# Windowed attention with a context prefix: the products across the border of the two token halves made for two heads at once

## The chip, the core and the metric

The kernel runs on one core of one Trainium2 chip. The core's engines work side by side and wait for each other through semaphores: PE multiplies matrices (PEld is the loading of its stationary operand), DVE and ACT work element by element and can read PE's results, POOL works element by element on the on-chip memory alone, and SP issues most of the DMAs. The metric is the device time of one execution in microseconds (us).

## The reference

Two layers run over 1,024 latent tokens of width 1,024 and 256 context tokens: an attention layer, then a convolution layer, then a final norm. The change lies in the attention layer, whose core is this:

```python
def windowed_attention(q, k, v, kc, vc, sink):
    # 16 query heads, 4 key/value heads, head width 128, WINDOW = BLOCK = 128
    ...
    def block_fn(args):
        qblk, blk = args                       # one block of 128 queries
        kw = lax.dynamic_slice_in_dim(kp, start, span, axis=1)   # keys of 3 blocks
        vw = lax.dynamic_slice_in_dim(vp, start, span, axis=1)
        ...
        p_ctx, p_win = sink_softmax(sink_l, s_ctx, s_win)
        o = (jnp.einsum('bhgqc,bchd->bqhgd', p_ctx.astype(vc.dtype), vc)
             + jnp.einsum('bhgqk,bkhd->bqhgd', p_win.astype(vw.dtype), vw))
        return o
    ...
y = (o * jax.nn.silu(z)) @ w_out
```

A block of 128 queries reads the key blocks before it, at it and behind it, and all 256 context keys, in one softmax with a sink. The result is multiplied by a gate made from z before the output projection.

## The kernel before

Every fp32 operand is held as two parts, a rounded high part and the rest as low part, and a product is three matmuls: high by high, low by high, high by low. All matmuls of the attention are issued in the order in which the program is written; the instructions of the other engines, SP's DMA issues among them, are ordered by a scheduler.

The attention walks 128 steps, 16 heads (h) by 8 query blocks (qb). In a step PE makes the scores of the next step (`scores`, L1035), then a fixed number of matmuls of other work, usually 12 (`fill`, L1022: projections of later heads, at the end the first rows of the output projection), then, where one is queued, a product of probabilities and values (`pv`, L1090), then the transposes of this step's probabilities (`transposes`, L1069). Between `scores` and `transposes` the softmax runs on the other engines: DVE takes scores, mask and maximum into p, ACT the exponential, DVE the reciprocal, POOL scales p.

`transposes` leaves the probability blocks, keys in the partitions, in two buffers of 22 blocks of 128 columns: `pthi` (high parts, written by ACT) and `ptlo` (low parts, DVE). They serve one token half, that is 4 query blocks, at a time, and the next half writes over them.

`pv(h, half)` multiplies the blocks of one half by the values. It makes seven products of three matmuls each, all into one PSUM bank (`pso`, 512 columns): two for the context, 512 columns wide; four for the half's own key blocks, 256 or 384 wide; and one for the key block just across the border between the halves. That last one concerns one query block alone, 128 columns. It is made 256 wide: the query block's probabilities stand beside a block of `pthi` and `ptlo` that was set to zero at the program's start (blocks 0 and 21). DVE then multiplies the bank by the gate into `oz`, and SP stores 512 columns to `ozd` in DRAM. The half 0 of a head is queued after step qb = 3 and made in step 4; the half 1 is made in step 0 of the next head. Where the next head begins a new group of four, keys and values are made first and `pv(h, 1)` stands behind them (L1220 on).

The output projection (`proj_attn`, L720) reads `ozd` back in rows of two heads (`ozf`, split by ACT into `ozh` and by DVE into `ozl`) with the weights `wo` and `wol`. The first `EARLY_ROWS` = 7 rows are begun for two token blocks inside the last head's steps; `ahead` (L753) loads up to `EA` = 2 rows ahead.

Tiles of 1,024 words come from a list of 45 pages that are handed out in the order in which they were freed (`Pages`). Operations are recorded through one helper, so the profile puts nearly all of them on L89; they are told apart by the names of their tiles.

Of the kernel before, what the change touches and what calls it, by code (L numbers as in the profile page):

```python
# [19 lines left out]
NH = 16  # L20
# [74 lines left out]
def backbone_kernel(  # L95
# [526 lines left out]
    anchor = []  # L622
    anchor_p = []
    anchor_a = []

    def after(ins, anchor=anchor):
        if anchor:
# [92 lines left out]
    def proj_attn():  # L720

        st, oz = {}, {}
        todo = {"load": 0, "split": 0}

        def load(i):
            s, kk = seqB[i]
            h, m = subs[s]
            w, wl = pg.alloc(F32, [2, 512], "wo"), pg.alloc(F32R, [2, 512], "wol")
            SY.dma_start(out=w, in_=pair_rows(Wo, m, kk))
            SY.dma_start(out=wl.bitcast(F32), in_=wolA[m, kk])  # L730
            st[i] = [w, wl]
            if m == 0:
                f = pg.alloc(F32, [2, 512], "ozf")
                SY.dma_start(out=f, in_=ozd[2 * kk:2 * kk + 2, :, h * 512:h * 512 + 512].rearrange("a p n -> p a n"))
                oz[(h, kk)] = f

        def split(i):
            s, kk = seqB[i]
            h, m = subs[s]
            w, wl = st[i]  # L740
            wh = pg.alloc(F32R, [2, 512], "woh")
            act(wh, w, AF.Copy)
            pg.free(w)
            st[i] = (wh, wl)
            if m == 0:
                f = oz[(h, kk)]
                oh, ol = pg.alloc(F32R, [2, 512], "ozh"), pg.alloc(F32R, [2, 512], "ozl")
                act(oh, f, AF.Copy)
                split_lo(V, ol, f, oh)
# [186 lines left out]
    def finish(kind, n, half, o, d, ropes=None, hold=None):  # L936
# [10 lines left out]
        if kind in "qk":  # L947
            return rope(o, sl, d, ropes, hold)
        if kind == "z":
            act(d[:, sl], o, AF.Tanh, scale=0.5)  # L950
            stt(d[:, sl], d[:, sl], 1.0, o, ALU.add, ALU.mult)
            return None
        w = CT if half == 2 else 512
        f = hp.alloc(F32, None, "vf")
# [80 lines left out]
    def scores(h, qb):  # L1035
# [29 lines left out]
        V.reciprocal(ri, l0)  # L1065
        anchor_p[:] = [G.tensor_scalar(out=p[:, 0:w], in0=p[:, 0:w], scalar1=ri, scalar2=1.0, op0=ALU.mult, op1=ALU.mult)]
        ptile[(h, qb)] = p

    def transposes(h, qb):  # L1069
        p = ptile.pop((h, qb))  # L1070
# [1 line left out]
        nb = k1 - k0 + 1  # L1072
        tb = ps_s()
        ql = qb % 4
        rels = []
        for kb in range(k1, k0 - 1, -1):
            rel = 1 - (kb - qb)
            rels.append(rel)
            PE.transpose(tb[:, rel * P:(rel + 1) * P], p[:, (kb - k0) * P:(kb - k0 + 1) * P], ident)
        for i in range(2):  # L1080
            PE.transpose(tb[:, (3 + i) * P:(4 + i) * P], p[:, (nb + i) * P:(nb + i + 1) * P], ident)
# [8 lines left out]
    def pv(h, half):  # L1090
        g = h // 4
        c, vh, vl = kvt[g][2:5]
        o = ps_o(0)
        q0 = half * 4
        work = [(*(c[:, n, i * P:i * P + P] for n in (2, 3)), slice(13 + 4 * i, 17 + 4 * i), slice(0, 512)) for i in range(2)]
        for kb in range(max(q0 - 1, 0), min(q0 + 4, TB - 1) + 1):
            qa, qz = max(kb - 1, q0), min(kb + 1, q0 + 3)
            b0 = 1 + 4 * (1 - (kb - qa)) + (qa - q0)
            n = qz - qa + 1
            if n == 1 and kb > qa:  # L1100
                work.append((vh[:, kb], vl[:, kb], slice(0, 5, 4), slice(256, 512)))
            elif n == 1:
                work.append((vh[:, kb], vl[:, kb], slice(9, 22, 12), slice(0, 256)))
            else:
                work.append((vh[:, kb], vl[:, kb], slice(b0, b0 + 5 * (n - 1) + 1, 5),
                             slice((qa - q0) * P, (qz - q0 + 1) * P)))
        for n, (a, b, ps_, os_) in enumerate(work):
            last = n == len(work) - 1
            PE.matmul(o[:, os_], a, pthi[:, ps_], start=n == 0, stop=False)
            PE.matmul(o[:, os_], a, ptlo[:, ps_], start=False, stop=False)  # L1110
            PE.matmul(o[:, os_], b, pthi[:, ps_], start=False, stop=last)
        sl = slice(half * 512, half * 512 + 512)
        oz = hp.alloc(F32, None, "oz")
        stt(oz[:, 0:512], o, 0.5, zt[h][:, sl], ALU.mult, ALU.mult)
        SY.dma_start(out=ozd[h, :, sl], in_=oz[:, 0:512])
        hp.free(oz)
        if half:
            pg.free(zt.pop(h))
            pg.free(*qt.pop(h))

    d0 = [target("k", 0), [], []]
    tails = []
# [73 lines left out]
    for i, (h, qb) in enumerate(steps):  # L1196
# [22 lines left out]
        if regroup:  # L1219
# [3 lines left out]
            transposes(h, qb)  # L1223
            run(job(("v", g)))
            pv(h, 1)
            pg.free(*old)
            scores(*nxt)
            vlate.pop(g)()
            continue
# [14 lines left out]
    pg.free(*kvt[NG - 1])  # L1244
    pg.free(mask_pg)


# [624 lines left out]
```

## Time and profile before

| | us |
|---|---|
| median of 3 runs | 1698.68 |
| lowest and highest of them | 1698.52 and 1701.01 |
| the profiled execution's own time | 1698.45 |
| its span in the trace | 1696.5 |

In the profile, rows of grouped instructions give line, engine, operation, tiles (written from read), shape and count, then the busy time in us and the mean duration of one in ns, then the engine's idle time before them and what ended it. Rows of the timeline give the start in us, the duration, and the instruction. A matmul's duration runs from its start to its modelled end; matmuls overlap, so the duration of one is longer than the distance to the next.

### The profile page before, as it was taken

The numbers are of one execution on the slowest core, as the hardware profiler recorded it, in microseconds if no ns is written. First come the engines' busy times: TensorE is split into PE (matmuls) and PEld (weight loads), VectorE is DVE, ScalarE is ACT, GpSimd is POOL, SyncE is SP. The second block draws the span as 40 slices with busy tenths as digits, with TensorE's granted clock in tenths as the row PEclk, the third lists the DMA queues.
The fourth block names the chain that finished last, engine by engine and source line by source line (L and its number), as shares of the span: only waits on it lengthen the run. The fifth ranks groups of instructions, "written<-read, shape, count | busy, mean of one in ns | idle before, by whom it ended". The sixth has DMA issues, their size and how long they took to land.

```text
span 1696.5 us, 23980 instructions
## 1 busy us (share of the span) xinstructions
PE 1682.6 (99%) x8484; PEld 1419.0 (84%) x8484; DVE 1088.4 (64%) x2068; ACT 877.4 (52%) x1540; POOL 880.8 (52%) x730
## 2 busy tenths in 40 slices
PE   9999999999999999999999999999999999999998
PEld 6788888888888888888888888888888888888886
DVE  5755544555355544556215289999999999867832
ACT  5745543555355544546234355665665664566741
POOL 0255663666556663653001167999898888130400
PEclk9999999999999999999999999999999999999999
DMA  9424442444335443437776623010111202377881
GB/s 386 147 82 134 158 122 94 134 143 152 97 119 160 149 134 93 140 120 279 269 253 219 234 81 100 13 63 26 63 62 44 88 32 81 125 267 247 312 296 50
DMA packets 110424, 244.55 MB, mean 144 GB/s; under 512 B 11370, under 2 KB 28066, under 8 KB 110304
## 3 DMA queue, kind: packets, MB, share of 16 engines
q1 hardware_dynamic: 104224, 233.05, 40.4%
q10 hardware_dynamic: 6080, 9.97, 2.3%
q8 instruction: 67, 1.10, 0.3%
q14 instruction: 53, 0.43, 0.1%
HBM read 190.80 MB, written 41.69 MB: 137 GB/s over the span
## 4 chain that ended last, share of the span: by engine, by line
PE 94%; DMA 3%; DVE 1%; POOL 1%; ACT 1%; issue 0%; SPq 0%; ACTq 0%; POOLq 0%
PE psg L89 49%; PE pss L89 24%; PE pso L89 21%; DMA x_page<-in_x_dram 1%; DMA rope_half<-rope_half 1%; DMA x_page<-in_ctx_dram 1%; DMA araw_page<-in_k_ada_dram 1%; DVE hf_page L89 0%; POOL rope_half L89 0%; DMA dww_raw<-in_ada_w_dram 0%; POOL wlo_page L89 0%; ACT x_page L89 0%; ACT hh_page L89 0%; DVE hl_page L89 0%; POOL ql_page L89 0%
## 5 line engine op out<-in xcount | busy, mean ns | idle before, releaser
L89 POOL TENSOR_TENSOR odd_half<-odd_half,prod_half 128x513 f32<-128x513 f32 (+2 forms) x252 | 314.1, 1253 | 22.7 <-ACT prod_half L89 9.4
L89 PE MATMUL psg<-hh_page,whi_page 128*128 128x512 f32 x600 | 235.5, 393 | 0.0
L89 PE MATMUL psg<-hl_page,whi_page 128*128 128x512 f32 x600 | 234.4, 391 | 0.0
L89 PE MATMUL psg<-hh_page,wlo_page 128*128 128x512 f32 x600 | 234.0, 390 | 0.0
L89 POOL TENSOR_TENSOR wlo_page<-wraw_page,whi_page 128x512 fp32r<-128x512 f32 (+1 forms) x104 | 173.0, 1678 | 106.7 <-ACT whi_page L89 55.9
L89 ACT ACTIVATE prod_half<-ubuf,dww 128x513 f32<-128x513 f32 (+2 forms) x252 | 165.5, 675 | 116.4 <-POOL odd_half L89 112.5
L89 PE MATMUL psg<-h2h_page,whi_page 128*128 128x512 f32 x464 | 181.9, 392 | 0.0
L89 PE MATMUL psg<-h2h_page,wlo_page 128*128 128x512 f32 x464 | 180.6, 389 | 0.0
L89 PE MATMUL psg<-h2l_page,whi_page 128*128 128x512 f32 x464 | 180.6, 389 | 0.0
L89 POOL TENSOR_SCALAR p_page<-p_page,sc 128x640 f32<-128x640 f32 (+1 forms) x128 | 99.2, 775 | 143.2 <-DVE sc L89 135.1
L89 DVE SCALAR_TENSOR_TENSOR pss<-ubuf,dww,pss 128x512 f32<-128x512 f32 (+3 forms) x270 | 172.3, 670 | 0.1
L89 DVE SCALAR_TENSOR_TENSOR pss<-ubuf,wsum,pss 128x512 f32<-128x512 f32 (+3 forms) x270 | 171.7, 670 | 0.2
L89 ACT ACTIVATE pthi<-pss 128x640 fp32r<-128x640 f32 (+1 forms) x144 | 89.2, 619 | 140.1 <-PE pss L89 130.1
L89 DVE TENSOR_TENSOR ptlo<-pss,pthi 128x640 fp32r<-128x640 f32 (+1 forms) x144 | 103.3, 718 | 82.4 <-ACT pthi L89 81.9
L89 ACT ACTIVATE p_page<-p_page,sc 128x641 f32<-128x641 f32 (+1 forms) x128 | 102.8, 803 | 70.1 <-DVE sc L89 67.5
L89 PEld LDWEIGHTS psg<-hh_page,wlo_page 128*128 128x128 f32 x600 | 112.7, 188 | 24.5
L89 POOL TENSOR_TENSOR rope_half<-rope_half,sin_page 128x512 f32<-128x512 f32 x40 | 52.9, 1322 | 153.3 <-DMA rope_half<-rope_half 147.1
L89 PEld LDWEIGHTS psg<-hh_page,whi_page 128*128 128x128 f32 x600 | 112.7, 188 | 19.3
L89 PEld LDWEIGHTS psg<-hl_page,whi_page 128*128 128x128 f32 x600 | 112.8, 188 | 18.4
L89 ACT ACTIVATE whi_page<-wraw_page 128x1024 fp32r<-128x1024 f32 x88 | 92.6, 1052 | 54.2 <-PE psg L89 21.0
L89 PE MATMUL pso<-h2l_page,whi_page 128*128 128x512 f32 x304 | 118.3, 389 | 0.0
L89 PE MATMUL pso<-h2h_page,wlo_page 128*128 128x512 f32 x304 | 118.3, 389 | 0.0
(255 smaller groups left out, 4056.0 us busy)
## 6 DMA issues: line engine op xcount, KB each, us to landing
wraw_page<-in_k_wconv_dram SPq DMA_DIRECT2D x48, 512.0 KB, 3.3
wraw_page<-in_k_win_dram SPq DMA_DIRECT2D x40, 512.0 KB, 3.4
wol_page<-wolA SPq DMA_DIRECT2D x32, 512.0 KB, 6.2
wo_page<-in_attn_w_out_dram SPq DMA_DIRECT2D x32, 512.0 KB, 6.0
wo_page<-in_conv_w_out_dram SPq DMA_DIRECT2D x32, 512.0 KB, 6.3
wol_page<-wolC SPq DMA_DIRECT2D x32, 512.0 KB, 6.1
rope_half<-rope_half ACTq DMA_DIRECT2D x76, 128.0 KB, 3.2
araw_page<-in_k_ada_dram SPq DMA_DIRECT2D x16, 512.0 KB, 11.0
```

Source lines behind the costliest of these rows:

```text
L89: r = f(*a, **k)
```

## The change

- The border product leaves `pv`, which then has six products, and no zero blocks are needed. For each pair of heads (2n, 2n + 1) one new function, `pv_shared`, makes the border products of both heads and both directions: key block 4 with the query blocks 3 of both heads (256 columns), and key block 3 with the query blocks 4 of both heads (256 columns). It stands in step qb = 2 of the next pair's even head, and for the last pair behind the last `pv`.
- For that the even head's border blocks are kept in blocks 20 and 21 of `pthi` and `ptlo` until the odd head's are there, in blocks 3 and 16. The other blocks are laid out anew, so that the two-piece copy of step qb = 0 becomes one piece, and that of the even head's steps 3 and 4 becomes two.
- `pv` stores 384 columns to `ozd` in place of 512. The 128 columns of the border block, which lack the products across the border, are copied by DVE into a page (`ozs`, 1,024 words), and ACT copies the gate's columns of the two border blocks of a head there too. `pv_shared` multiplies its bank by these gate columns (two DVE operations of 128 by 256), adds the kept sums (one of 128 by 512), and stores 256 columns for each of the two heads.
- Pages: one more is held for a pair's sums and gates; a group's two value pages are freed two steps later; a head's two query pages are freed earlier, in the last `scores` of the head.
- In the output projection the early rows no longer load rows 7 and 8, since row 7 reads heads 14 and 15, whose border columns are stored last. The splits of `ozf` in later rows are ordered behind the last gate computation (`anchor_z`).

The diff, cut:

```diff
-    for t in (pthi, ptlo):
-        for b in (0, 21):
-            V.tensor_copy(t[:, b], zer[:, 0:P])
...
-            ahead(i, EA, min(1, EARLY_ROWS - 1 - i))
+            ahead(i, min(EA, EARLY_ROWS - 1 - i), min(1, EARLY_ROWS - 1 - i))
...
-        for r0, r1 in (((0, 2), (3, 5)) if qb == 0 else ((1, 5),) if qb == TB - 1 else ((0, 5),)):
-            b0 = 1 + ql + 4 * r0
-            bs = slice(b0, b0 + 4 * (r1 - r0 - 1) + 1, 4)
+        a0, a1 = int(qb == TB - 1), 4 if qb == 0 else 5
+        runs = [(a0, a1, slice(ql + 4 * a0, ql + 4 * a1 - 3, 4))]
+        if h % 2 == 0 and qb == 3:
+            runs = [(1, 5, slice(7, 20, 4)), (0, 1, slice(20, 21))]
+        elif h % 2 == 0 and qb == 4:
+            runs = [(0, 4, slice(0, 13, 4)), (4, 5, slice(21, 22))]
+        for r0, r1, bs in runs:
             anchor_a[:] = [act(pthi[:, bs], tv[:, r0:r1], AF.Copy)]
+        for r0, r1, bs in runs:
             anchor[:] = [split_lo(V, ptlo[:, bs], tv[:, r0:r1], pthi[:, bs])]
...
-        for kb in range(max(q0 - 1, 0), min(q0 + 4, TB - 1) + 1):
+        for kb in range(q0, q0 + 4):
...
-            if n == 1 and kb > qa:
-                work.append((vh[:, kb], vl[:, kb], slice(0, 5, 4), slice(256, 512)))
-            elif n == 1:
-                work.append((vh[:, kb], vl[:, kb], slice(9, 22, 12), slice(0, 256)))
...
-        SY.dma_start(out=ozd[h, :, sl], in_=oz[:, 0:512])
+        stt(oz[:, 0:512], o, 0.5, zv, ALU.mult, ALU.mult)
+        V.tensor_copy(part[:, e0:e0 + 128], oz[:, edge])
+        SY.dma_start(out=ozd[h, :, sl][:, own], in_=oz[:, own])
         hp.free(oz)
         if half:
+            act(part[:, 768 - 256 * (h % 2):1024 - 256 * (h % 2)], zt[h][:, 384:640], AF.Copy)
             pg.free(zt.pop(h))
...
+    def pv_shared(h):
+        vh, vl = kvt[h // 4][3:5]
+        o = ps_o(0)
+        pv_mm(o[:, 0:256], [(vh[:, 4], vl[:, 4], slice(3, 21, 17), slice(0, 256))])
+        pv_mm(o[:, 256:512], [(vh[:, 3], vl[:, 3], slice(16, 22, 5), slice(0, 256))])
+        part = shared.pop()
+        oz = hp.alloc(F32, None, "oz")
...
+        for e in range(2):
+            stt(sv[:, e], ov[:, e], 0.5, zv[:, e], ALU.mult, ALU.mult)
+        tt(V, oz[:, 0:512], oz[:, 0:512], part[:, 0:512], ALU.add)
+        for e in range(2):
+            SY.dma_start(out=ozd[h - e, :, 384:640].rearrange("p (q n) -> p q n", q=2), in_=sv[:, e])
...
+        if qb == 1 and h and h % 2 == 0:
+            pvq.append((h - 1, 2))
...
+    fill(12)
+    pv(NH - 1, 2)
     fill(1000)
```

What it does to the order of instructions is shown at three places. On PE, the end of one `pv` (head 4, half 0; `pso` is its bank, `vh` and `vl` the values' two parts), before:

```order
L89 MATMUL pso_2978<-pthi,vh_page_2619 128x384
L89 MATMUL pso_2978<-ptlo,vh_page_2619 128x384
L89 MATMUL pso_2978<-pthi,vl_page_2620 128x384
L89 MATMUL pso_2978<-pthi,vh_page_2619 128x256
L89 MATMUL pso_2978<-ptlo,vh_page_2619 128x256
L89 MATMUL pso_2978<-pthi,vl_page_2620 128x256
L89 MATMUL pso_2978<-pthi,vh_page_2619 128x256
L89 MATMUL pso_2978<-ptlo,vh_page_2619 128x256
L89 MATMUL pso_2978<-pthi,vl_page_2620 128x256
```

and now the new product of heads 2 and 3, two steps ahead of that place, between the fill and the transposes of its step:

```order
L89 MATMUL psg_2840<-hl_page_500,whi_page_2646 128x512
L89 MATMUL psg_2840<-hh_page_499,wlo_page_2647 128x512
L89 MATMUL pso_2890<-pthi,vh_page_777 128x256
L89 MATMUL pso_2890<-ptlo,vh_page_777 128x256
L89 MATMUL pso_2890<-pthi,vl_page_778 128x256
L89 MATMUL pso_2890<-pthi,vh_page_777 128x256
L89 MATMUL pso_2890<-ptlo,vh_page_777 128x256
L89 MATMUL pso_2890<-pthi,vl_page_778 128x256
L89 MATMUL pss_2903<-ident,p_page_2815 128x128 x5
```

Each of the 32 `pv` has lost three rows of 256 columns, the border product (last in half 0, first behind the context in half 1), and each of the 8 pairs has gained six; nothing else on PE has changed its place.

On POOL, around the scaling of head 2, step 3 (`p_page`; `wlo` is the low part of a projection weight that the scheduler put in between, `low` that of an output weight), before:

```order
L89 TENSOR_SCALAR p_page_1812<-p_page_1812,sc_1813 128x640
L89 TENSOR_TENSOR wlo_page_1948<-wraw_page_1541,whi_page_1947 128x512 x2
L89 TENSOR_SCALAR p_page_1853<-p_page_1853,sc_1854 128x640
L89 TENSOR_TENSOR low_page_1839<-low_page_1839,lhi_page_1389 128x512
L89 TENSOR_SCALAR p_page_1896<-p_page_1896,sc_1897 128x640
```

and now:

```order
L89 TENSOR_TENSOR low_page_1674<-low_page_1674,lhi_page_1383 128x512
L89 TENSOR_SCALAR p_page_1801<-p_page_1801,sc_1802 128x640
L89 TENSOR_SCALAR p_page_1842<-p_page_1842,sc_1843 128x640
L89 TENSOR_TENSOR wlo_page_1952<-wraw_page_1535,whi_page_1951 128x512 x2
L89 TENSOR_TENSOR low_page_1828<-low_page_1828,lhi_page_1383 128x512
```

The two halves of the weight's low part now stand behind the scaling of step 3 and no longer ahead of it.

On SP, at the end of the attention (`oz_half` is what a `pv` leaves, `ozf` what a row of the output projection reads), before:

```order
L89 DMA ozf_page_8074<-ozd 128x2x512
L89 DMA wol_page_8286<-wolA 128x1024
L89 DMA dwr_page_8139<-in_conv_dw_w_dram 31x1024
L89 DMA gate_page_8136<-gd_603 128x1024
L89 DMA wo_page_8285<-in_attn_w_out_dram 128x2x512
L89 DMA wo_page_8465<-in_attn_w_out_dram 128x2x512
L89 DMA ozd<-oz_half_8116 128x512
L89 DMA xr_page_8470<-in_x_dram 128x512 x2
```

and now:

```order
L89 DMA ozd<-oz_half_8155 128x384
L89 DMA wol_page_8324<-wolA 128x1024
L89 DMA ozd<-oz_half_8179 128x2x128 x2
L89 DMA wo_page_8323<-in_attn_w_out_dram 128x2x512
L89 DMA ozf_page_8309<-ozd 128x2x512
L89 DMA wo_page_8405<-in_attn_w_out_dram 128x2x512
L89 DMA xr_page_8530<-in_x_dram 128x512 x2
```

The load of row 7's input (the `ozf` row of each) stood ahead of the last store of the attention; it now stands behind the two stores of the last pair's border columns, which it needs.

More of the change, by code (lines that the diff above doesn't have):

```diff
@@ L624, in backbone_kernel @@
     anchor_a = []
+    anchor_z = []
     def after(ins, anchor=anchor):
@@ L747, in split @@
                 oh, ol = pg.alloc(F32R, [2, 512], "ozh"), pg.alloc(F32R, [2, 512], "ozl")
-                act(oh, f, AF.Copy)
-                split_lo(V, ol, f, oh)
+                after(act(oh, f, AF.Copy), anchor_z[0:1] if i else [])
+                after(split_lo(V, ol, f, oh), anchor_z[1:2] if i else [])
                 pg.free(f)
@@ L1067, in scores @@
         ptile[(h, qb)] = p
+        if qb == TB - 1:
+            pg.free(*qt.pop(h))
     def transposes(h, qb):
@@ L1074, in transposes @@
         ql = qb % 4
-        rels = []
         for kb in range(k1, k0 - 1, -1):
-            rel = 1 - (kb - qb)
-            rels.append(rel)
-            PE.transpose(tb[:, rel * P:(rel + 1) * P], p[:, (kb - k0) * P:(kb - k0 + 1) * P], ident)
+            at = 2 - 2 * (kb - qb)
+            PE.transpose(tb[:, at * P:(at + 1) * P], p[:, (kb - k0) * P:(kb - k0 + 1) * P], ident)
         for i in range(2):
-            PE.transpose(tb[:, (3 + i) * P:(4 + i) * P], p[:, (nb + i) * P:(nb + i + 1) * P], ident)
+            at = 1 + 2 * i
@@ L1087, in transposes @@
+        for r0, r1, bs in runs:
             anchor_a[:] = [act(pthi[:, bs], tv[:, r0:r1], AF.Copy)]
+        for r0, r1, bs in runs:
             anchor[:] = [split_lo(V, ptlo[:, bs], tv[:, r0:r1], pthi[:, bs])]
[L1090 to L1095, printed above, removed]
-        for kb in range(max(q0 - 1, 0), min(q0 + 4, TB - 1) + 1):
-            qa, qz = max(kb - 1, q0), min(kb + 1, q0 + 3)
-            b0 = 1 + 4 * (1 - (kb - qa)) + (qa - q0)
-            n = qz - qa + 1
-            if n == 1 and kb > qa:
-                work.append((vh[:, kb], vl[:, kb], slice(0, 5, 4), slice(256, 512)))
-            elif n == 1:
-                work.append((vh[:, kb], vl[:, kb], slice(9, 22, 12), slice(0, 256)))
-            else:
-                work.append((vh[:, kb], vl[:, kb], slice(b0, b0 + 5 * (n - 1) + 1, 5),
-                             slice((qa - q0) * P, (qz - q0 + 1) * P)))
+    shared = []
@@ L1107, in pv, with pv_mm @@
+    def pv_mm(o, work):
         for n, (a, b, ps_, os_) in enumerate(work):
@@ L1111, in pv @@
             PE.matmul(o[:, os_], b, pthi[:, ps_], start=False, stop=last)
+    def pv(h, half):
+        if half == 2:
+            return pv_shared(h)
+        c, vh, vl = kvt[h // 4][2:5]
+        o = ps_o(0)
+        q0 = half * 4
+        work = [(*(c[:, n, i * P:i * P + P] for n in (2, 3)), slice(4 + 8 * i, 8 + 8 * i), slice(0, 512)) for i in range(2)]
+        for kb in range(q0, q0 + 4):
+            qa, qz = max(kb - 1, q0), min(kb + 1, q0 + 3)
+            b0 = qa - q0 + 8 * (qa - kb + 1)
+            work.append((vh[:, kb], vl[:, kb], slice(b0, b0 + 9 * (qz - qa) + 1, 9), slice((qa - q0) * P, (qz - q0 + 1) * P)))
+        pv_mm(o, work)
@@ L1112, in pv @@
         sl = slice(half * 512, half * 512 + 512)
+        if h % 2 == 0 and half == 0:
+            shared[:] = [pg.alloc(F32, [1024], "ozs")]
+        part = shared[0]
         oz = hp.alloc(F32, None, "oz")
-        stt(oz[:, 0:512], o, 0.5, zt[h][:, sl], ALU.mult, ALU.mult)
-        SY.dma_start(out=ozd[h, :, sl], in_=oz[:, 0:512])
+        own, edge = (slice(128, 512), slice(0, 128)) if half else (slice(0, 384), slice(384, 512))
+        zv = zt[h][:, sl]
+        e0 = 256 * half + 128 * (1 - h % 2)
@@ L1116, in pv @@
+        stt(oz[:, 0:512], o, 0.5, zv, ALU.mult, ALU.mult)
+        V.tensor_copy(part[:, e0:e0 + 128], oz[:, edge])
+        SY.dma_start(out=ozd[h, :, sl][:, own], in_=oz[:, own])
         hp.free(oz)
         if half:
+            act(part[:, 768 - 256 * (h % 2):1024 - 256 * (h % 2)], zt[h][:, 384:640], AF.Copy)
             pg.free(zt.pop(h))
-            pg.free(*qt.pop(h))
+    def pv_shared(h):
+        vh, vl = kvt[h // 4][3:5]
+        o = ps_o(0)
+        pv_mm(o[:, 0:256], [(vh[:, 4], vl[:, 4], slice(3, 21, 17), slice(0, 256))])
+        pv_mm(o[:, 256:512], [(vh[:, 3], vl[:, 3], slice(16, 22, 5), slice(0, 256))])
+        part = shared.pop()
+        oz = hp.alloc(F32, None, "oz")
+        ov, sv, pv_ = (t[:, 0:512].rearrange("p (q e n) -> p e q n", q=2, e=2) for t in (o, oz, part))
+        zv = part[:, 512:1024].rearrange("p (e q n) -> p e q n", q=2, e=2)
+        for e in range(2):
[3 more added lines that the diff above has]
+            SY.dma_start(out=ozd[h - e, :, 384:640].rearrange("p (q n) -> p q n", q=2), in_=sv[:, e])
+        hp.free(oz)
+        pg.free(part)
+        if h % 4 == 3:
+            pg.free(vh, vl)
@@ L1225, in backbone_kernel @@
             pv(h, 1)
-            pg.free(*old)
+            pg.free(*old[:3])
             scores(*nxt)
@@ L1242, in backbone_kernel @@
         pv(*pvq.popleft())
+    fill(12)
+    pv(NH - 1, 2)
     fill(1000)
-    pg.free(*kvt[NG - 1])
+    pg.free(*kvt[NG - 1][:3])
     pg.free(mask_pg)
```

4 lines of the change are left out of this document (2 added, 2 removed).

## The prediction

> **What bounds the kernel now.** I read the page first: the share of each engine and the chain of work that ended last.
>
> ```profile
> span 1696.5 us, 23980 instructions
> PE 1682.6 (99%) x8484; PEld 1419.0 (84%) x8484; DVE 1088.4 (64%) x2068; ACT 877.4 (52%) x1540; POOL 880.8 (52%) x730
> ...
> PE 94%; DMA 3%; DVE 1%; POOL 1%; ACT 1%; issue 0%; SPq 0%; ACTq 0%; POOLq 0%
> ```
>
> PE is on the chain for 94% of the span. A busy PE need not be a bound one, so the second view is that of the waits, for PE alone (engine, what waited, for whom: us in total, times, longest):
>
> ```profile
> PE pss L89 <- DVE zerr_page L89: 2.0, 1, 2.0
> PE psg L89 <- DVE rope_half L89: 1.4, 2, 1.1
> ...
> PE pso L89 <- DVE oz_half L89: 0.5, 3, 0.2
> ```
>
> The first is the start-up's. The other two, 1.9 us together, are all that matters here: in the attention PE hardly waits. The third view, busy time by stretch (attention, output projection, convolution), says whether another engine is close behind (columns: stretch, its length, then PE, PEld, DVE, ACT and POOL busy, granted clock, DMA share, GB/s):
>
> ```profile
> 100.00:825.00 725.00, 723.09 (x4021) 628.91 (x4020) 370.87 (x818) 354.39 (x741) 396.50 (x368) 1.00 0.44 140
> 825.00:870.00 45.00, 45.00 (x209) 36.87 (x208) 7.21 (x17) 14.35 (x19) 2.97 (x2) 1.00 0.78 260
> ...
> 1100.00:1500.00 400.00, 400.00 (x1773) 331.10 (x1772) 387.75 (x591) 235.20 (x321) 316.45 (x217) 1.00 0.21 69
> ```
>
> In the attention the other engines are busy for half of the time or a little more, so PE work that is removed there is time. DVE is close behind only in the convolution (387.75 of 400), whose work the change leaves as it is: it starts earlier and runs as before.
>
> **What is removed.** The border product is three matmuls in each of 32 `pv`, 96 in all; the 8 shared products bring back six each, 48. So 48 matmuls of 256 columns go. Their price is not the duration in the grouped rows:
>
> ```profile
> L89 PE MATMUL pso<-ptlo,vh_page 128*128 128x256 f32 x96 | 26.9, 281 | 0.0
> L89 PE MATMUL pso<-pthi,vl_page 128*128 128x256 f32 x96 | 26.9, 281 | 0.0
> ```
>
> 281 ns is start to modelled end, and neighbours overlap. What PE's line advances by is the distance from start to start, in the timeline of one `pv`:
>
> ```profile
> 165.05 0.28 PE L89 MATMUL pso<-pthi,vh_page 128*128 128x256 f32 x1
> 165.16 0.28 PE L89 MATMUL pso<-ptlo,vh_page 128*128 128x256 f32 x1
> 165.28 0.28 PE L89 MATMUL pso<-pthi,vl_page 128*128 128x256 f32 x1
> 165.40 0.28 PE L89 MATMUL pso<-pthi,vh_page 128*128 128x256 f32 x1
> 165.51 0.28 PE L89 MATMUL pso<-ptlo,vh_page 128*128 128x256 f32 x1
> 165.63 0.28 PE L89 MATMUL pso<-pthi,vl_page 128*128 128x256 f32 x1
> 165.75 0.34 PE L89 MATMUL pso<-pthi,vh_page 128*128 128x384 f32 x1
> ```
>
> Six of them take 165.75 − 165.05 = 0.70 us, 0.117 each. The last three are such a padded border product, so the price is that of the very form. 48 x 0.117 = **5.6 us** off PE's line. (By durations it would be 48 x 0.281 = 13.5, which PE's own line contradicts.)
>
> **What is added beside it.** Rows for the new operations, the nearest ones:
>
> ```profile
> L89 DVE SCALAR_TENSOR_TENSOR pso<-wsum_raw,cs,pso 128x256 f32<-128x256 f32 x64 | 30.7, 480 | 3.3 <-DMA wsum_raw<-in_ada_w_dram 3.2
> L89 DVE TENSOR_TENSOR x_page<-x_page,xr_page 128x512 f32<-128x512 f32 x20 | 14.9, 743 | 0.3
> L89 DVE COPY mask_page<-pso 128x256 f32<-128x256 f32 x16 | 6.7, 420 | 0.2
> L89 DVE TENSOR_TENSOR ptlo<-pss,pthi 128x640 fp32r<-128x640 f32 x96 | 78.8, 821 | 57.8 <-ACT pthi L89 57.5
> L89 DVE TENSOR_TENSOR ptlo<-pss,pthi 128x256 fp32r<-128x256 f32 x32 | 13.5, 421 | 6.9 <-ACT pthi L89 6.6
> L89 DVE TENSOR_TENSOR ptlo<-pss,pthi 128x512 fp32r<-128x512 f32 x16 | 11.0, 690 | 17.8 <-ACT pthi L89 17.8
> L89 ACT ACTIVATE pthi<-pss 128x256 fp32r<-128x256 f32 x32 | 12.3, 384 | 29.9 <-PE pss L89 23.6 <-DVE ptlo L89 6.3
> ```
>
> DVE, for a pair: four copies of 128 columns, at most 0.42 each (a row of twice the width), 1.7; two gate products, 2 x 0.48, and one addition, 0.74, together 1.70; the splits of step 0 in one piece, 0.69 for 2 x 0.42, save 0.15 for each of two heads; those of the even head's steps 3 and 4 in two pieces, 0.69 + at most 0.42 for 0.82, cost 0.29 each. Sum about 3.7 us, 8 pairs 29 us, beside 371 of 725. ACT gets two gate copies of 0.38 a pair and like changes of its splits, some 8 us in all, beside 354. SP gets 16 more stores of the same bytes. None of this is on PE's line as long as the softmax of the next step is done in time.
>
> That cover has to be looked at where it is thinnest. A step's transposes wait for POOL's scaling of p, and the new DVE work stands in step 2 of even heads, ahead of the transposes of step 3. Two such places, head 2 and head 6, POOL and PE:
>
> ```profile
> 175.85 2.56 POOL L89 TENSOR_TENSOR wlo_page<-wraw_page,whi_page 128x512 fp32r<-128x512 f32 x2 [4.07 <-ACT whi_page L89]
> 178.38 0.81 POOL L89 TENSOR_SCALAR p_page<-p_page,sc 128x640 f32<-128x640 f32 x1
> ...
> 366.91 0.81 POOL L89 TENSOR_SCALAR p_page<-p_page,sc 128x640 f32<-128x640 f32 x1 [1.40 <-DVE sc L89]
> ```
>
> ```profile
> 179.53 0.71 PE L89 MATMUL pss<-ident,p_page 128*128 128x128 f32 x5
> ...
> 370.49 0.71 PE L89 MATMUL pss<-ident,p_page 128*128 128x128 f32 x5
> ```
>
> At head 6 the scaling ended at 367.72 and its transposes began at 370.49: 2.8 us to spare, against 1.70 us of new DVE work less the 0.70 us by which PE's own step grows. At head 2 it ended at 179.19, only 0.34 us ahead, because the two weight parts of 2.56 us stood before it; the new order puts them behind that scaling, so the margin grows there. Bounds of this term: nothing where the margin holds, 1.70 − 0.70 − 0.34 = 0.66 us a pair where it is the thin one. I take four waits of the size that PE already shows for such an evacuation (0.5 us in 3): **0.7 us**.
>
> **The end of the attention** is the second place. Row 7 of the output projection now reads columns that the last shared product makes, so its load can no longer stand ahead. The chain: DVE 1.70, store, load, ACT split, DVE split, then PE. Rows (the second view is that of the tile between 780 and 850 us):
>
> ```profile
> ozd<-oz_half SPq DMA_DIRECT2D x32, 256.0 KB, 4.2
> ```
>
> ```profile
> L89 ACT ACTIVATE ozh_page<-ozf_page x6: 1046/1059/1062, 785.2 to 817.9; 128x1024 fp32r<-128x1024 f32 x6
> L89 DVE TENSOR_TENSOR ozl_page<-ozf_page,ozh_page x6: 1215/1225/1233, 786.3 to 819.9; 128x1024 fp32r<-128x1024 f32 x6
> ...
> DMA to landing us min/median/max: 8.8/9.5/10.1
> ```
>
> 1.70 + 4.2 + 9.5 + 1.06 + 1.23 = 17.7 us. Its cover is what PE has left between the end of the early rows and row 7:
>
> ```profile
> 822.48 0.39 PE L89 MATMUL pss<-woh_page,ozh_page 128*128 128x512 f32 x1
> ```
>
> ```profile
> 843.19 0.39 PE L89 MATMUL psg<-woh_page,ozh_page 128*128 128x512 f32 x1
> ```
>
> 20.7 us. That holds by 3 us, so this edit costs nothing. Without cover: if the store took as long as the slowest load, 10.1, and the load too, the chain is 24.2 and PE waits 3.5 us. Behind the store on SP wait the loads of row 8's weight and of later rows; row 8 comes 24 matmuls after row 7, at 20.7 us for 84 (7 rows x 2 blocks x 6) 5.9 us at most, so row 7 decides.
>
> The pages are one short at most (counted through the code's allocations, the fewest free at the start of a step are 2 where they were 3), the query pages come back earlier, and the zero fill at the start stands beside PE's start-up. I cost these at nothing; should a score step have to wait for a page, it shows as a wait of the first kind.
>
> **Sum**, against the profiled execution's own 1698.45 (span 1696.5 and 1.95 around it): 1698.45 − 5.6 + 0.7 = 1693.5. The median of the runs stands 0.2 above that execution, so I predict **1693.8**.
>
> **Rivals.**
>
> *The softmax chain gives part back* (0.08). Say the thin margin of 0.34 us were met at three pairs, each paying 0.66 for the shared product and 0.42 + 0.29 for copy and split in step 4: 4.1 us, time 1698.68 − 5.6 + 4.1 = 1697.2. For it: the scheduler has moved POOL, DVE and ACT all through the attention. Against: where I looked, the move went the right way.
>
> *Row 7 waits* (0.12): 3.5 us at the output projection, 1693.8 + 3.5 = 1697.3. For it: the DMA share there is 0.78. Against: it needs the store to be slower than any row shows.
>
> *DVE's new work collides with POOL* (0.06), the one that ends slower. The additions and copies read the on-chip memory alone, as POOL does, and the trace has an operation of that kind that takes longer beside POOL:
>
> ```profile
> L89 DVE TENSOR_TENSOR rope_half<-rope_half,rope_half 128x512 f32<-128x512 f32 x6 | 7.3, 1223 | 1.1 <-POOL rope_half L89 1.1
> ```
>
> 1223 for 743 ns is 0.48 us more, on DVE or on POOL. Five such operations a pair, 2.4 us, and the 0.66 + 0.71 from above make 3.8 us a pair at thin margins. From 9.0 / 8 = 1.13 us a pair (5.6 + 3.4) it is slower; at 1.5 us a pair the time is 1698.7 − 5.6 + 12 = 1705. Against: a margin like head 6's swallows most of it.
>
> The Trainium skill, "SBUF — State Buffer", section "SBUF: two separate sides", says that DVE and POOL share one pair of ports as an exclusive lock, held for a whole instruction, by a DVE operation with two inputs there or in a two-port mode. By that rule the copies too would hold POOL off, whose scaling is what the transposes wait for. The 1223 ns agree with it; the 743 ns show that a free POOL costs nothing.
>
> *The change does not take the matmuls away* (0.02): no change, 1698.7. The order on PE speaks against it.
>
> **Chances.** The forecast has 0.72. About 0.2% (3.4 us) is what a measurement of this kernel can tell from no change. Faster by more: 0.72 and 0.08 of the two partial cases, since their lower parts cost under 2 us: 0.80. Within it: the other 0.12 of them and the last rival, 0.14. Slower: 0.06. The range reaches from 1691.8 (5.6 off, the 1.1 us rope wait gone too, and 0.2 for a median's spread) to 1697.5, which holds both partial cases; the forecast's own is 1692.5 to 1695.2.
>
> **What would show it.** PE: 48 matmuls fewer, the rows `pso<-pthi,vh_page` 128x256 at x80 (96 − 32 + 16), 0.117 us apart. Right also if PE's waits in the attention stay near 2 us and the first matmul of row 7 follows its neighbour without a gap. Wrong if PE waits for POOL or DVE at the transposes of steps 3 and 4 of even heads, or for ACT at row 7, or if the two-input additions take near 1.2 us while scalings of p come late.

## The result, and the profile after

| | before | after | repeated beside two of the experiments |
|---|---|---|---|
| median of the runs, us | 1699.09 (6 runs) | 1693.84 (6 runs) | 1693.47 (6 runs), before 1698.50 |
| lowest and highest, us | 1698.46 and 1701.01 | 1691.36 and 1694.15 | 1692.03 and 1694.05 |
| ratio to before, 95% interval | | 0.9965 (0.9955 to 0.9975) | 0.9969 (0.9958 to 0.9981) |
| profiled execution, us (span) | 1698.45 (1696.5) | 1694.15 (1692.4) | 1694.05 (1692.2) |

The kernel is faster by 5.25 us; 4.9 us were predicted (1693.8). Between the two profiled executions the difference is 4.3 us. First the page of after, its span, the engines' busy time and the shares of the chain that ended last:

```profile
span 1692.4 us, 23973 instructions
PE 1676.4 (99%) x8436; PEld 1414.4 (84%) x8436; DVE 1115.4 (66%) x2120; ACT 880.9 (52%) x1556; POOL 881.3 (52%) x730
...
PE 92%; DMA 4%; DVE 2%; ACT 1%; issue 0%; SPq 0%; POOL 0%; ACTq 0%; DVEq 0%; POOLq 0%
```

There are 48 PE instructions fewer (8484 to 8436), and DVE is 27 us busier, where 29 were predicted. PE's waits after:

```profile
PE pss L89 <- DVE zerr_page L89: 2.0, 1, 2.0
PE pso L89 <- DVE dww L89: 1.4, 1, 1.4
PE pss L89 <- DVE hl_page L89: 1.2, 3, 0.6
PE pss L89 <- DVE ptlo L89: 1.1, 1, 1.1
...
PE pso L89 <- DVE oz_half L89: 0.5, 3, 0.2
PE psg L89 <- DVE zs_page L89: 0.4, 1, 0.4
```

Compared with before, `rope_half` (1.4 us) has vanished. New are `ptlo`, the low part of the probabilities in head 15, `dww`, copies of the convolution's taps that PE transposes within the output projection, and a little for `zs_page`, the last head's gate. None of them is in a place that the prediction watched. The groups, by shape:

```profile
L89 PE MATMUL pso<-pthi,vh_page 128*128 128x256 f32 x80 | 22.4, 280 | 0.0
...
L89 DVE COPY ozs_page<-oz_half 128x128 f32<-128x128 f32 x32 | 19.3, 603 | 1.2
L89 ACT ACTIVATE ozs_page<-zs_page 128x256 f32<-128x256 f32 x16 | 6.6, 412 | 0.2
L89 DVE SCALAR_TENSOR_TENSOR oz_half<-pso,ozs_page 128x256 f32<-128x256 f32 x16 | 6.0, 420 | 7.6 <-PE pso L89 7.6
L89 DVE TENSOR_TENSOR oz_half<-oz_half,ozs_page 128x512 f32<-128x512 f32 x8 | 5.5, 689 | 0.1
```

80 matmuls of 256 columns as predicted. The copies of border sums take 603 ns in the mean, where 420 had been set as the most; the gate products and additions on DVE cost a little less than they were given (420 and 689 ns for 480 and 743). The two stretches that answer to those shown of before (attention, output projection):

```profile
100.00:821.00 721.00, 718.83 (x3981) 625.69 (x3980) 396.58 (x874) 356.39 (x756) 397.01 (x368) 1.00 0.45 139
821.00:866.00 45.00, 43.64 (x203) 35.68 (x202) 8.29 (x18) 15.06 (x20) 2.96 (x2) 1.00 0.83 290
```

PE had no gap in the 45 us of the output projection before; now 1.4 us are missing. Where the time went shows best in PE's lead, the start of one and the same PE instruction before less after, in the two timelines:

| place | lead, us | what lies in between |
|---|---|---|
| first transposes of head 0 | −0.1 | |
| of head 15 | 7.6 | 48 matmuls at 0.117: 5.6; rope waits gone: 1.9; two short waits for POOL gone: 0.4, two new: −0.6; 0.4 in distances of 0.1 or less |
| first matmul of the projection behind the attention | 6.0 | waits in head 15: 1.6 |
| row 7 | 4.5 | wait for the taps: 1.5 |
| last matmul | 4.4 | |

The second row contains the vanished rope waits: PE's step from one matmul to the next was 1.39 us longer at 250 us than the same step after, and 0.49 at 442 us. It was waiting for DVE's multiplication, which empties the bank. That row of the kernel before, and the same one after (in brackets DVE's idle time ahead of it and what released it):

```profile
250.81 0.69 DVE L89 TENSOR_TENSOR rope_half<-psg,cos_page 128x512 f32<-128x512 f32 x1 [5.92 <-POOL ql_page L89]
```

```profile
245.91 0.69 DVE L89 TENSOR_TENSOR rope_half<-psg,cos_page 128x512 f32<-128x512 f32 x1 [4.62 <-ACT rope_half L89]
```

Before, it was released by POOL, at the end of another head's work; now by ACT's own part of the same rope. POOL was late there, with two parts of a weight, 2.54 us, between its multiplication (243.23) and its addition for that other head, before:

```profile
244.48 2.54 POOL L89 TENSOR_TENSOR wlo_page<-wraw_page,whi_page 128x512 fp32r<-128x512 f32 x2
246.98 1.29 POOL L89 TENSOR_TENSOR rope_half<-rope_half,rope_half 128x512 f32<-128x512 f32 x1
```

It was the same at 435.14. In the changed kernel the addition begins right behind the multiplication (239.97 and 241.33, 429.17 and 430.54). So the new order on POOL goes with this 1.9 us, which belongs to no term of the sum.

### The profile page after: what moved, and what is told of

Read it like the earlier page. It is cut to its first block, busy times and chain, and to the rows that moved or that the text cites. A ratio compares the mean times of both kernels' runs of the same rounds, so it can differ in the third digit from the quotient of the medians.

```text
span 1692.4 us, 23973 instructions
## 1 busy us (share of the span) xinstructions
PE 1676.4 (99%) x8436; PEld 1414.4 (84%) x8436; DVE 1115.4 (66%) x2120; ACT 880.9 (52%) x1556; POOL 881.3 (52%) x730
## 4 chain that ended last, share of the span: by engine, by line
PE 92%; DMA 4%; DVE 2%; ACT 1%; issue 0%; SPq 0%; POOL 0%; ACTq 0%; DVEq 0%; POOLq 0%
PE psg L89 49%; PE pss L89 23%; PE pso L89 21%; DMA x_page<-in_x_dram 1%; DMA x_page<-in_ctx_dram 1%; DMA araw_page<-in_k_ada_dram 1%; DMA wo_page<-in_attn_w_out_dram 0%; DMA rope_half<-rope_half 0%; DMA ozf_page<-ozd 0%; DVE hf_page L89 0%; DMA dww_raw<-in_ada_w_dram 0%; DVE ozl_page L89 0%; DVE oz_half L89 0%; ACT x_page L89 0%; ACT hh_page L89 0%
## 5 line engine op out<-in xcount | busy, mean ns | idle before, releaser
L89 ACT ACTIVATE pthi<-pss 128x512 fp32r<-128x512 f32 (+2 forms) x144 | 87.4, 618 | 111.6 <-PE pss L89 108.0
L89 DVE TENSOR_TENSOR ptlo<-pss,pthi 128x512 fp32r<-128x512 f32 (+2 forms) x144 | 101.9, 716 | 63.0 <-ACT pthi L89 61.7
L89 PE MATMUL pso<-h2h_page,whi_page 128*128 128x512 f32 x304 | 118.4, 389 | 0.0
```

Source lines behind the costliest of these rows:

```text
L89: r = f(*a, **k)
```

## The experiments

### What a border matmul is worth

The kernel before without its border products:

```diff
-        for kb in range(max(q0 - 1, 0), min(q0 + 4, TB - 1) + 1):
+        for kb in range(q0, q0 + 4):
```

> The kernel before without its border products: 96 matmuls of 256 columns are left out, so the output lacks the terms of the keys across the border between the token halves; nothing else differs. Theory (a removed border matmul is worth its start-to-start distance, 0.117 us, and nothing else is near the path in the attention): 96 x 0.117 = 11.2 us less than before, about 1687.5 us. Rival 1 (a matmul is worth its duration of 0.281 us): 27.0 us less, about 1672. Rival 2 (another engine or the softmax chain is close behind): clearly less than 11.2 us saved, with new waits of PE for DVE, ACT or POOL in the attention, some 1690 to 1694 us.

Measured: 1690.15 us (4 runs) against 1699.15, that is 9.0 us less; ratio 0.9949 (0.9936 to 0.9963). Durations as a price are refuted. Where nothing waits, between heads 4 and 7, PE's lead grows by 0.71 us a head of six matmuls, 0.119 each, which is the start-to-start price. Of the missing 2.2 us, 1.7 are in the waits:

```profile
PE psg L89 <- DVE rope_half L89: 2.3, 2, 1.8
...
PE pss L89 <- POOL p_page L89: 0.8, 2, 0.4
```

0.9 us more for the rope, 0.8 us for POOL's scaling of p. So the second rival has a part in it: at twice the dose the chain behind PE begins to show. One of the two waits for POOL is at 178.7 us, step 3 of head 2, where the prediction had found the thin margin of 0.34 us. A faster PE meets it; the new DVE work is not in this kernel.

The changed kernel with the shared products made twice, 48 matmuls back:

```diff
+        for _ in range(2):
             pv_mm(o[:, 0:256], [(vh[:, 4], vl[:, 4], slice(3, 21, 17), slice(0, 256))])
             pv_mm(o[:, 256:512], [(vh[:, 3], vl[:, 3], slice(16, 22, 5), slice(0, 256))])
```

> The changed kernel with every shared product made twice, the second time over the first: 48 matmuls of 256 columns more, the same output, the number of matmuls of the kernel before. Theory (what was gained is the 48 matmuls' start-to-start time): 5.6 us more than the changed kernel, about 1699.4 us, so the kernel before within 0.7 us. Rival 1 (part of the gain came from the new order: a vanished rope wait, later loads): less than the kernel before by 2 us or more, some 1696 us, the added matmuls then filling waits. Rival 2 (the PE steps of the pairs already wait for the softmax chain, so added PE work is partly free): under 4 us more than the changed kernel.

Measured: 1698.97 us (11 runs), ratio to before 1.0000 (0.9991 to 1.0009), 5.1 us above the changed kernel. The gain is that of the 48 matmuls. The first rival (some 1696 us) is refuted as far as the whole goes; in its trace the rope wait (1.9 us by the distances) stays away and others have come (1.6 us), which nearly cancel it:

```profile
PE pso L89 <- DVE dww L89: 0.8, 1, 0.8
...
PE pss L89 <- DVE ptlo L89: 0.3, 1, 0.3
```

### The wait for the taps

What happens in the output projection of the changed kernel, DVE first and then PE:

```profile
817.49 0.69 DVE L89 TENSOR_TENSOR oz_half<-oz_half,ozs_page 128x512 f32<-128x512 f32 x1
828.31 1.23 DVE L89 TENSOR_TENSOR ozl_page<-ozf_page,ozh_page 128x1024 fp32r<-128x1024 f32 x1 [10.12 <-ACT ozh_page L89]
829.45 0.47 DVE L89 COPY dww<-pso 128x124 f32<-128x124 f32 x2
```

```profile
828.04 0.39 PE L89 MATMUL pss<-woh_page,ozl_page 128*128 128x512 f32 x1
829.78 0.68 PE L89 MATMUL pso<-ident,dwr_page 32*128 32x32 f32 x8 [1.36 <-DVE dww L89]
```

DVE's queue goes in order. After the last shared product it stands 10.12 us at the split of row 7, which waits through ACT for the store and the load, and the tap copies stand behind it. PE's second group of tap transposes needs the banks that these copies empty. Row 7 itself is split by 829.54, 9 us before PE reads it (838.7). This was tried by moving one operation:

```diff
+                if i == EARLY_ROWS:
+                    split_lo(G, ol, f, oh)
+                else:
                     after(split_lo(V, ol, f, oh), anchor_z[1:2] if i else [])
```

> The changed kernel with one operation moved: the low-part split of row 7 (the first late row of the output projection) runs on POOL instead of DVE. Theory (PE's new wait of 1.4 us at 828 us is for the tap copies, which stand in DVE's queue behind that split, which waits 10 us for the late load): the wait is gone, row 7 begins with its neighbours, and the time is about 1.4 us below the changed kernel, near 1692.4 us. Rival 1 (the late load itself is what PE waits for): the wait stays as it is, the time is the changed kernel's. Rival 2 (what is behind it on POOL is wanted instead): a new wait of PE for POOL in its place, the same time or more.

Measured: 1692.58 us (5 runs) against 1699.15, and once more 1692.86 (5 runs) against 1698.77: 6.6 and 5.9 us below before, where the changed kernel stands 5.25 and 5.03 below. The wait for `dww` is gone from the list of both runs. That is about 1.1 us, and the intervals of the ratios, 0.9961 (0.9948 to 0.9973) and 0.9964 (0.9952 to 0.9977), overlap with the changed kernel's, so the trace carries this point: between the start of the projection and row 7 PE gains 1.45 us on the changed kernel's. The size of the wait varies with the load and with how late PE comes: in the six profiles of kernels that have the shared products and this split on DVE it is 1.4, 1.0, 0.8 and 0.5 us and twice nothing; in all five with the split on POOL there is none. The expectation of the second run:

> The changed kernel with row 7's low-part split on POOL, once more, beside the next kernel. Theory: near 1692.5 us as it was; PE waits once for the low part of p, 1.1 to 1.6 us at 787 or 791 us, and not for the tap copies.

As to the low part of p it was wrong in part: that run's profile has it twice, 1.1 and 1.5 us. It is taken up below.

Whether the late load alone would do it was asked of the kernel before:

```diff
-            ahead(i, EA, min(1, EARLY_ROWS - 1 - i))
+            ahead(i, min(EA, EARLY_ROWS - 1 - i), min(1, EARLY_ROWS - 1 - i))
```

> The kernel before with one edit of the change alone: the loads of late projection rows no longer stand ahead of the early rows; border products as before. Theory (the tap wait of 1.4 us needs both the late load and the shared product that makes the row's last columns late; here those columns are long stored when the load is issued): the time of the kernel before within 0.5 us, no wait of PE for the tap copies. Rival (the late load alone puts the split behind PE's need): a wait of PE of 1 to 2 us for the tap copies near 834 us, about 1.4 us more than the kernel before, 1700.5 us.

Measured: 1698.93 us (11 runs) against 1699.16, ratio 0.9998 (0.9989 to 1.0007), and no wait for the taps. As the theory has it, the late load and the late columns must come together.

### The copies that take longer

> The changed kernel with the border sums put into the page by a second multiplication straight from the product's bank, in place of a copy from the on-chip memory to itself. Theory (the copies' mean of 603 ns, with a median of 228 and a longest of 1351, comes from a collision with POOL's two-input operations, and costs PE nothing since it lies under PE's steps): the new operations take about 280 ns each with little spread, DVE is busy some 10 us less over the 32 of them, and the time is within 0.5 us of the changed kernel. Rival (the collision holds PE up at the next splits): up to 1 us less, and shorter waits of PE for DVE in the attention.

```diff
-        V.tensor_copy(part[:, e0:e0 + 128], oz[:, edge])
+        stt(part[:, e0:e0 + 128], o[:, edge], 0.5, zv[:, edge], ALU.mult, ALU.mult)
```

In the changed kernel, one of the long copies (DVE) and POOL at the same time:

```profile
187.01 1.27 DVE L89 COPY ozs_page<-oz_half 128x128 f32<-128x128 f32 x1
```

```profile
186.92 1.29 POOL L89 TENSOR_TENSOR rope_half<-rope_half,sin_page 128x512 f32<-128x512 f32 x1 [1.97 <-DMA rope_half<-rope_half]
```

The copy begins while POOL works and ends 0.08 us behind POOL's instruction. Of the 32 copies, the 17 that no POOL instruction overlaps take 222 to 229 ns. The second multiplication instead, which reads PSUM:

```profile
L89 DVE SCALAR_TENSOR_TENSOR ozs_page<-pso,zs_page x32: 278/280/283, 107.4 to 815.7; 128x128 f32<-128x128 f32 x32
...
PE pso L89: 1.1, 3
```

280 ns and no spread, beside POOL too: the theory holds, and DVE saves 19.3 − 9.0 = 10.3 us. PE gains nothing by it: 1694.20 us (6 runs), ratio to before 0.9969 (0.9957 to 0.9981). It waits 1.1 us in three places for the bank, which is read twice now, where it waited 0.5 us. The trace shows no tap wait, but the copies are not the reason: row 7's load landed earlier. ACT's split began 4.5 us after the load's issue, and 6.1 us in the changed kernel.

### The wait in head 15

```profile
784.85 2.36 DVE L89 TENSOR_TENSOR ozl_page<-ozf_page,ozh_page 128x1024 fp32r<-128x1024 f32 x2
787.12 0.82 DVE L89 TENSOR_TENSOR ptlo<-pss,pthi 128x640 fp32r<-128x640 f32 x1
```

These are DVE's rows of the changed kernel. The low part of p stands behind two splits of rows of the output projection, of which PE needs the first at 789.4 and the second (row 4) at 804.4 us. ACT had the high part ready at 785.9. The first attempt dropped the ordering edge:

```diff
-                after(act(oh, f, AF.Copy), anchor_z[0:1] if i else [])
-                after(split_lo(V, ol, f, oh), anchor_z[1:2] if i else [])
+                act(oh, f, AF.Copy)
+                split_lo(V, ol, f, oh)
```

> The changed kernel without the ordering edge that holds the splits of the early projection rows back until the gate columns of the last head are made; same work, same values. Theory (PE's new wait of 1.1 us at 787 us is for the low part of p, which stands in DVE's queue behind two such splits of 1.22 us each): the two splits fall into DVE's idle 2.3 us at 780.5 us, the wait is gone, the time is about 1.1 us below the changed kernel, near 1692.7 us. Rival 1 (the low part is late by itself, for ACT's high part): the wait stays at 1.1 us and so does the time. Rival 2 (the loads of these rows are not there yet): DVE waits for them in its queue, PE's wait grows, 1 us or more above the changed kernel.

Measured: 1695.30 us (11 runs) against 1699.16, ratio 0.9978 (0.9969 to 0.9987): 3.9 us below before, where the changed kernel stands 5.25 and 5.03 below, so it is slower by 1.2 to 1.4 us. The theory's remedy fell, and the second rival was right. ACT and DVE stood in their queues for a load that had not landed, ahead of the gate that PE needs:

```profile
782.60 1.06 ACT L89 ACTIVATE ozh_page<-ozf_page 128x1024 fp32r<-128x1024 f32 x1 [1.45 <-DMA ozf_page<-ozd]
```

```profile
PE psg L89 <- DVE zs_page L89: 2.6, 1, 2.6
```

The wait costs more than its length. The stretch just behind it, with the granted clock third from the end:

```profile
787.00:790.00 3.00, 3.00 (x9) 2.31 (x10) 3.00 (x5) 2.01 (x4) 0.03 (x1) 0.51 1.04 409
```

Matmuls of 512 columns stand 0.43 us apart there in place of 0.23, and PE loses another 1.5 us. Behind the wait of 1.4 us in the changed kernel the clock is 1.00.

The two edits together fare the same (3.1 us at `zs_page` by the start-to-start distances, then a clock of 0.50), 1695.53 us (9 runs), ratio 0.9977 (0.9968 to 0.9987):

> The changed kernel with both edits: no ordering edge on the early rows' splits, and row 7's low-part split on POOL. Theory (the waits of 1.1 and 1.4 us are separate, each one is a place in DVE's queue): both are gone, 2.5 us below the changed kernel, near 1691.3 us. Rival (the time won at 787 us only makes PE wait longer at 828 us or later, for the store and load of row 7, which hang on the last shared product): only one of the two is won, near 1692.5 us.

The second attempt moved row 4's split to POOL (`G if i in (4,) else V`), beside the changed kernel itself, and with row 7's there too (`(4, EARLY_ROWS)`):

> The changed kernel as it is, on the chip and in the rounds of the next two, so that differences of about one us can be told. Both theories: near 1693.8 us, waits of PE of 1.1 us for the low part of p and up to 1.4 us for the tap copies.

> The changed kernel with the low-part split of the fifth early projection row on POOL instead of DVE, the ordering edge kept. Theory (PE's wait of 1.1 us near 787 us is for the low part of p behind two splits in DVE's queue, and only this second one is needed late): one split of 1.22 us less stands ahead, the wait falls to 0.2 us or less, about 1.0 us below the changed kernel, near 1692.8 us, less what row 7's load then makes PE wait longer (0 to 1 us). Rival (POOL's own work, the scalings of p, comes late behind the split of about 2.4 us): a wait of PE for POOL of about 1 us in its place, the same time.

> The changed kernel with two low-part splits on POOL instead of DVE: of the fifth early projection row and of row 7. Theory (the two new waits are separate places in DVE's queue): both gone, about 2.4 us below the changed kernel, near 1691.4 us. Rival (PE, earlier by 1.1 us, then waits for row 7's store and load themselves): only 1.2 to 1.4 us below, near 1692.5 us.

Measured: 1693.47 (6 runs), 1693.87 (10 runs) and 1692.63 us (5 runs), against 1698.50. So row 4 on POOL gives nothing, and the pair gives only what row 7 gave. In the traces of both the wait stands at 791 or 792 us and is no shorter (1.6 us); in the repetition of the changed kernel, too, most of it was there (1.1 us, and 0.3 at 787). Why POOL does not help is seen in DVE and POOL of the kernel with both rows there:

```profile
786.65 2.53 DVE L89 TENSOR_TENSOR ozl_page<-ozf_page,ozh_page 128x1024 fp32r<-128x1024 f32 x1
```

```profile
785.17 2.94 POOL L89 TENSOR_TENSOR ozl_page<-ozf_page,ozh_page 128x1024 fp32r<-128x1024 f32 x1 [1.38 <-ACT ozh_page L89]
```

DVE's next split, 1.22 us by itself, takes 2.53: it ends 1.07 us behind POOL's. What was taken out of DVE's queue came back into it as a collision, ahead of the next low part. Neither the theory nor the rival of that expectation had this. The profile with row 4 alone on POOL has no wait for the taps; it is one of the two with an early load (4.8 us from issue to ACT's split), and its PE came later.

The third attempt leaves the work on DVE and orders each early row's split behind the low part of p of its own step, with row 7 on POOL:

```diff
-                after(split_lo(V, ol, f, oh), anchor_z[1:2] if i else [])
+                lo = split_lo(G if i == EARLY_ROWS else V, ol, f, oh)
+                after(lo, anchor if 2 <= i < EARLY_ROWS else anchor_z[1:2] if i else [])
```

> The changed kernel with row 7's low-part split on POOL, and the splits of early rows 2 to 6 ordered on DVE behind the low part of p of their own step instead of behind the gate columns alone; same work. Theory (PE's wait in head 15 is one stretch of DVE's queue, in which splits not needed for up to 16 us stand ahead of the low part of p): no wait for the low part of p above 0.3 us, 1.1 to 1.6 us below the kernel with row 7 on POOL alone, near 1691.2 us. Rival (the DVE stretch is simply full, so that what is put later is late there): waits of PE for the rows' low parts between 796 and 815 us in its place, the same time.

Measured: **1691.16 us** (5 runs, 1690.89 to 1692.10) against 1692.86 (1692.38 to 1693.81) of the kernel with row 7 on POOL alone, on the same chip; ratio to before 0.9954 (0.9940 to 0.9967). The runs of the two don't overlap. Its list of waits:

```profile
PE pss L89 <- DVE zerr_page L89: 2.0, 1, 2.0
PE pss L89 <- DVE hl_page L89: 1.2, 3, 0.6
PE pss L89 <- DVE x_page L89: 1.1, 1, 1.1
```

`ptlo` and `dww` are both gone, and no row came late: the splits stand where PE reads them next. This is the fastest version here, 7.6 us below before. PE's lead over the kernel with row 7 on POOL is 2.8 us at the end of the attention (there the low part of p was waited for twice, 1.1 and 1.5 us), and 1.3 at its last matmul. The wait for `x_page` behind the output projection is new in this profile. Its cause:

```profile
963.66 2.92 DVE L89 TENSOR_TENSOR x_page<-x_page,xr_page 128x512 f32<-128x512 f32 x1
```

```profile
963.62 7.68 POOL L89 TENSOR_TENSOR wlo_page<-wraw_page,whi_page 128x1024 fp32r<-128x1024 f32 x3 [28.99 <-DMA wraw_page<-in_k_wconv_dram]
```

POOL began 0.04 us ahead of DVE, and the addition took 2.92 us. In the kernel with row 7 alone DVE began 0.19 us ahead of POOL, and it took 0.69.

## Why the prediction was right, and where not

- **What is removed** was right in number and price: 48 matmuls, 5.6 us. The doubled product gave 5.1 us and the undisturbed heads 0.119 us a matmul. Durations would have said 13.5.
- **The softmax chain**, 0.7 us in four waits at the transposes of steps 3 and 4 of even heads, was set too high and sought in the wrong place. At those steps PE does not wait for the softmax. By the start distances the changed kernel has two waits for POOL at transposes, 0.2 us at 199 us and 0.4 at 724, and the kernel before had two of 0.2, at 139 and 220, which are gone: 0.1 us in sum (0.5 in the repetition). The new ones are at the last step of heads 2 and 13. What makes them is not DVE's new work but POOL's new order, two parts of a weight ahead of the scaling:

```profile
721.55 2.54 POOL L89 TENSOR_TENSOR wlo_page<-wraw_page,whi_page 128x512 fp32r<-128x512 f32 x2
724.09 0.69 POOL L89 TENSOR_SCALAR p_page<-p_page,sc 128x512 f32<-128x512 f32 x1
```

The rival that this chain gives much back did not happen.
- **The end of the attention, "so this edit costs nothing"**, is the step that failed most clearly. The chain itself kept inside its cover: from the gate products (816.70) to the split's end (829.54) it took 12.8 us, where 17.7 had been worked out, row 7 was ready 9 us early, and the rival "row 7 waits" did not happen either. What the step left out is who stands behind the waiting instruction on its engine. The prediction looked at SP's queue behind the store, and not at DVE's behind the split, where the tap copies stood: 1.4 us in this profile (1.0 in the repetition).
- **The early rows**: their new ordering was given no cost. It puts a split ahead of the low part of p in head 15. Ordered behind the low part, the splits cost nothing, which shows the cause. The price was 1.6 us between the two profiles of before and after.
- **The rope wait** was counted only at the low end of the range, as a possible gain. It came, with 1.9 us, and stands against the two above: 5.6 + 1.9 + 0.4 − 0.6 − 1.6 − 1.5 = 4.2 of the 4.5 us that PE gains from the first transposes to the last matmul; the rest is spread over distances of 0.1 us or less. So the 4.9 that were forecast came close by luck: errors of both signs cancel. That the new order on POOL brought the rope's gain was read from the traces (the kernel with the products doubled has it too), not tried alone.
- **The copies** were under-sized, 603 for at most 420 ns. That cost PE nothing, as the experiment on them showed.
- **The rival of the collision with POOL** had the right mechanism and, in the main, the wrong place. The copies suffer it. The additions take 0.69 us throughout, and one of the eight held POOL's scaling up: at 175.66 us it took 1.23 us for 0.80, and the step's margin covered that. In head 15 a split held a scaling up for longer:

```profile
789.56 1.70 POOL L89 TENSOR_SCALAR p_page<-p_page,sc 128x640 f32<-128x640 f32 x1 [0.87 <-DVE sc L89]
```

DVE's split, 1.19 us, had begun 0.17 us ahead of it.

## What to carry to other kernels

A matmul that is removed from a bound PE is worth its distance from start to start, and the doubled product is a cheap way to show it. For an instruction that now waits longer, read its whole queue: here the row that waited was in time, and an unrelated copy behind it was not. When a late operand is put into an in-order queue, order it behind what is wanted sooner; moving it to another engine only helps where the two don't meet at the on-chip memory.

## What the runs showed of the hardware

DVE and POOL shut each other out for whole instructions. On POOL a scaling took 1.70 us for 0.80 beside a split that DVE had begun 0.17 us ahead. On DVE a copy of 128x128 from the on-chip memory to itself takes 0.23 us alone and up to 1.35 beside POOL, ending with POOL's instruction; a two-input split took 2.53 for 1.22, an addition 2.92 for 0.69; a multiplication that takes one input from PSUM is untouched at 0.28 us, 17 of its 32 executions beside POOL. The Trainium skill, "SBUF — State Buffer", section "SBUF: two separate sides", describes this as an exclusive lock on a shared pair of ports, which goes to whichever began first; by that rule 0.04 us decide over 2.2, and the split and the addition that were shown agree with it.

PE's clock fell after long waits: behind waits of 2.6 and 2.9 us the granted clock was 0.51 and 0.50 over 3 us, behind one of 1.4 us it was 1.00.

The runs of one kernel scatter by 1 to 5 us, and part of it lies at the start: PE waited 0.2 us for the first weights (`araw_page`) in the profile of the changed kernel, and 1.7 in the first one with row 7 on POOL. So a difference of one us between two profiled executions says little, and the leads above are to be read from row to row.
